# Hybrid attention and state-space trunk on one core: background sums behind products of P and V, output-projection preparation behind the last softmax, two background steps a unit

## The chip, the core and the metric

One core of a Trainium2 chip runs the whole program: TensorE (PE, with weight loads as PEld), VectorE (DVE), ScalarE (ACT), GpSimd (POOL) and SyncE (SP), which issues most DMAs. The metric is the device time of one execution in microseconds. The kernel before took 2346.74 us (median of three runs, 2342.58 to 2348.49).

## What is computed

Two layers on 1024 tokens of 1024 features, everything in float32. Layer 0 mixes tokens by latent attention, layer 1 by a state-space model; each mixer and each feed-forward network is wrapped with a modulation that depends on one vector c.

```python
cs = silu(c)
for i in range(2):
    shift, scale, gate = modulation(cs, mod_mix_w[i], mod_mix_b[i])   # cs @ W + b, W 1024 x 3072
    y = mixer_i(x * (1 + scale) + shift)
    x = layer_norm(ALPHA * x + (1 + gate) * y, ln_mix_g[i], ln_mix_b[i])
    shift, scale, gate = modulation(cs, mod_ffn_w[i], mod_ffn_b[i])
    a = relu((x * (1 + scale) + shift) @ mlp_w1[i] + mlp_b1[i])       # 1024 -> 4096
    y = (a * a) @ mlp_w2[i] + mlp_b2[i]                               # 4096 -> 1024
    x = layer_norm(ALPHA * x + (1 + gate) * y, ln_ffn_g[i], ln_ffn_b[i])
```

In the attention of layer 0, `s = q k^T` is causal, `p = softmax(s)`, `o = p v` for 8 heads, and `o @ w_o` is the output projection. The change touches only this stage and the modulation work that runs beside it.

## The kernel before

Products of float32 accuracy are made of three TensorE products: each operand is split into a high and a low part (`split`, lines 73 to 75: ACT writes the high part, DVE subtracts for the low one), and `mm3` (lines 77 to 80) adds high by high, high by low, low by high in PSUM.

**Attention.** 16 units of work are walked in order: head h (8) by half I of the queries (2), four query tiles of 128 rows each. For unit n the loop at line 800 interleaves: the projections of Q and K of unit n + 2 (`proj`), the scores of unit n + 1 (`score`), the projection of V of unit n + 1 (`vproj`), and the product of P and V of unit n (`pv`). A score tile has up to 1024 columns; its softmax is a chain over engines: DVE adds the mask (line 750) and takes the maximum (752), ACT takes the exponential (754), DVE the reciprocal of the sum (755), ACT scales the tile in place (759; for the first two tiles of a head POOL does it, line 757). `pv` transposes the scaled tile on PE (770), ACT and DVE split it (774, 775), and three products per 128 keys (782) go into PSUM tile `o`. Projections, V and the sums named next share one PSUM tile `pj` with a single buffer (line 537).

**Background.** The modulation rows of later stages are made by a generator `bg` that runs beside attention: 8 halves of 512 columns, each as 8 loads of a 128x512 block (`mb`, line 572, two raw buffers), scaled and added on POOL (574, 576, 577) into an accumulator `acc` (two buffers, so half n + 2 overwrites half n). A step of the generator is two blocks. When a half is complete, `mod_end` adds the bias (591, rows only) and sums over partitions with ones on PE: one product for a row (594) and four products of one column each (602) for columns. Halves 0, 1 give the row `grow`, 2 to 5 columns, 6 and 7 the row `gffn`. The sum of a half is written one half later than its blocks. Line 819 takes 3 steps a unit (2 in the first three units).

**Output projection.** `out_weight` (921) loads the 8 blocks of `w_o` (`wor`, 512 KB each, two buffers) and splits them into `woh`, `wol`; `o_stage` (952) splits the attention output oT into `oh` for each token tile; `o_tiles` (930) multiplies, k outermost for the first two token tiles. Block k = 7 needs the last head, so it comes after the last product of P and V.

**Order.** The instructions are written in program order, and a scheduler puts them on each engine by a simulated time line; `tc.issue_after(x)` keeps what is written under it behind instruction x. Every engine, and the SP queue with its loads, then works in that fixed order.

Of the kernel before, what the change touches and what calls it, by code (L numbers as in the profile page):

```python
# [12 lines left out]
AF = mybir.ActivationFunctionType  # L13
# [26 lines left out]
def kernel(  # L40
# [13 lines left out]
    V, S, P, PE, SY = nc.vector, nc.scalar, nc.gpsimd, nc.tensor, nc.sync  # L54
# [22 lines left out]
    def mm3(ps, lh, ll, rh, rl, start, stop):  # L77
        PE.matmul(ps, lh, rh, start=start, stop=False)  # L78
        PE.matmul(ps, lh, rl, start=False, stop=False)  # L79
        PE.matmul(ps, ll, rh, start=False, stop=stop)  # L80

    cst = pool("cst")
    ident = cst.tile([128, 128], F32, name="ident")
# [1 line left out]
    ones = cst.tile([128, 128], F32, name="ones")  # L85
# [211 lines left out]
    ps = tr4()  # L297
# [172 lines left out]
    for v, vt in ((v1, vt1), (v2, vt2)):  # L470
        ps = tr4()
# [93 lines left out]
    def mod_block(wsrc, bsrc, bcols, m, kind, dst, psp, hv, drow=None, on_pool=False):  # L565

        for h in range(2):
# [14 lines left out]
            hv.flush()  # L582
            hv.pend.append(lambda h=h, acc=acc: mod_end(bsrc, bcols, m, h, kind, dst, psp, hv, acc, drow))

    def mod_end(bsrc, bcols, m, h, kind, dst, psp, hv, acc, drow):
        c0 = m * 1024 + h * 512
        sl = slice(h * 512, h * 512 + 512)
        if kind == "row":
            r = hv.raw()
            SY.dma_start(r[0:1], bsrc[c0:c0 + 512].unsqueeze(0))  # L590
            P.tensor_tensor(acc[0:1], acc[0:1], r[0:1], ALU.add)
        ps = psp()
        if kind == "row":
            PE.matmul(ps, ones, acc, start=True, stop=True)
            if drow is None:
                V.tensor_scalar(dst[:, sl], ps, 1.0, None, ALU.add)
            else:
                V.tensor_scalar(r[0:1], ps[0:1], 1.0, None, ALU.add)
                SY.dma_start(drow[:, sl], r[0:1])
        else:  # L600
            for k in range(4):
                PE.matmul(ps[:, k:k + 1], acc[:, k * 128:(k + 1) * 128], ones[:, 0:1], start=True, stop=True)
            ks = slice(4 * h, 4 * h + 4)
            V.scalar_tensor_tensor(dst[:, ks], ps[:, 0:4], 1.0 if m == 1 else 0.0, bcols[:, ks], ALU.add, ALU.add)

# [21 lines left out]
    def step(gen, n=1, late=0):  # L627
        if late:
            with tc.high_priority(offset=-late):
                step(gen, n)  # L630
            return
        for _ in range(n):
            next(gen, None)
# [3 lines left out]
    bg = chain(mod_block(mod_mix_w[0], mod_mix_b[0], None, 2, "row", grow, pj, hv, on_pool=True),  # L637
               mod_all(0, mod_ffn_w[0], mod_ffn_b[0], 48, 0, 0, gffn, pj, hv, on_pool=True), mod_flush(hv))
# [87 lines left out]
        yield  # L726

    PT = {}
    behind_ = []

    def score(h, i):
        I = i // 4
        w = (i + 1) * 128
        ps = ps_s[i % 2].tile([128, 1024], F32, tag="s", name="s")
        qsl = slice((i % 4) * 128, (i % 4) * 128 + 128)
        qh, ql = Q[h, I]
        st = ST[h, I]
        for cc in range((w + 511) // 512):
            n = min(512, w - 512 * cc)
            if n == 128:  # L740
                n = 256
            o = ps[:, 512 * cc:512 * cc + n]
            kh, kl = K_[h, cc]
            mm3(o, qh[:, qsl], ql[:, qsl], kh[:, 0:n], kl[:, 0:n], True, False)
            ks, kx = (kE, kO) if h % 2 == 0 else (kO, kE)
            ksl = slice(512 * cc, 512 * cc + n)
            PE.matmul(o, st[:, qsl], ks[:, ksl], start=False, stop=False)
            PE.matmul(o, st[:, qsl], kx[:, ksl], start=False, stop=True)
        d = ps[:, i * 128:i * 128 + 128]
        V.tensor_tensor(d, d, cmask, ALU.add)  # L750
        mx = ap3.tile([128, 16], F32, tag="mx", name="mx", bufs=4)
        V.reduce_max(mx[:, 1:2], ps[:, 0:w], axis=AX.X, negate=True)
        p = ap3.tile([128, w], F32, tag=f"p{i}", name="p", bufs=1)
        S.activation(p, ps[:, 0:w], AF.Exp, bias=mx[:, 1:2], scale=1.0, accum_out=mx[:, 2:3])
        V.reciprocal(mx[:, 3:4], mx[:, 2:3])
        if i < 2:
            behind_.append(P.tensor_scalar(p, p, mx[:, 3:4], 0.0, ALU.mult, ALU.add).ins)
        else:
            S.activation(p, p, AF.Copy, scale=mx[:, 3:4])
        PT[h, i] = p  # L760

    def pv(h, I):
        hp, hh = divmod(h, 2)
        o = ps_o.tile([128, 512], F32, tag="o", name="o")
        nk = 4 * I + 4
        for kt in range(nk):
            j0 = max(kt - 4 * I, 0)
            tp = tr4()
            for j in range(j0, 4):
                PE.transpose(tp[:, j * 128:j * 128 + 128], PT[h, 4 * I + j][:, kt * 128:kt * 128 + 128], ident)  # L770
            ph = ap3.tile([128, 512], F32R, tag="ph", name="ph", bufs=5)
            pl_ = ap3.tile([128, 512], F32R, tag="pl", name="pl", bufs=5)
            c0 = j0 * 128
            S.activation(ph[:, c0:512], tp[:, c0:512], AF.Copy)
            V.tensor_tensor(pl_[:, c0:512], tp[:, c0:512], f32(ph[:, c0:512]), ALU.subtract)
            if j0 == 3:
                c0 = 256
                V.memset(f32(ph[:, 256:384]), 0.0)
                V.memset(f32(pl_[:, 256:384]), 0.0)
            vh, vl = VV[hp, kt // 2]  # L780
            vsl = slice((kt % 2) * 256 + hh * 128, (kt % 2) * 256 + hh * 128 + 128)
            mm3(o[:, c0:512], vh[:, vsl], vl[:, vsl], ph[:, c0:512], pl_[:, c0:512], kt == 0, kt == nk - 1)
            yield
        S.activation(oT[I][:, h].rearrange("p (s n) -> p s n", s=8), o.rearrange("p (n s) -> p s n", s=8), AF.Copy)

# [14 lines left out]
    for n, (h, I) in enumerate(units):  # L800
        pr = proj(*units[n + 2]) if n + 2 < len(units) else iter(())
        vp = vproj(*units[n + 1]) if n + 1 < len(units) else iter(())
        pvg = pv(h, I)
        for i in range(4):
            s_ = 4 * n + 4 + i
            if s_ < len(tiles):
                if s_ // 4 == n + 2:
                    step(pr, 100)
                score(*tiles[s_])
            step(pvg, 1 if I == 0 else 2)  # L810
            step(pr)
            if i > 1:
                step(vp)
        step(pvg, 100)
        step(pr, 100)
        if n + 3 < len(units) and units[n + 3][0] % 2 == 0:
            qpe(units[n + 3][0] // 2, units[n + 3][1])
        with tc.issue_after(behind_[1]):
            step(bg, 3 if n > 2 else 2)
    step(bg, 100)  # L820
    for I in range(2):
        tap(f"oT{I}", oT[I])
    for p_ in (*ps_s[::-1], ps_o, ps_j, pt_, bg_p, ap3, ap2, ap1, mk, mp):
# [97 lines left out]
    def out_weight(wp, src, gate, k, hi, lo):  # L921

        r = wp.tile([128, 1024], F32, tag="wr", name="wor")
        d = SY.dma_start(r, src[k * 128:(k + 1) * 128, :])
        if gate is not None:
            V.tensor_tensor(r, r, gate, ALU.mult)
        split(hi, lo, r)
        return d.ins

    def o_tiles(lhs, w, k_outer=False):  # L930
# [4 lines left out]
        for i, hf, k in order:  # L935
# [5 lines left out]
    wp = pool("wp", bufs=2)  # L941
    wo_p = [pool(f"wo_p{i}") for i in range(3)]
    wo_k = [wo_p[0 if k < 2 else 1 if k < 7 else 2] for k in range(8)]
    WO = [(wo_k[k].tile([128, 1024], F32R, name=f"woh{k}"), wo_k[k].tile([128, 1024], F32R, name=f"wol{k}"))
          for k in range(8)]
    for k in range(8):
        out_weight(wp, mla_w_o[0], None, k, *WO[k])
    rb = res_row(wp, ln_mix_b[0], gb2=(gffn, mlp_b2[0]))
    tok = lambda ap: ap[0].rearrange("(n t) d -> t n d", t=8)
    xr = tok(x)  # L950
# [1 line left out]
    def o_stage(t):  # L952

        if t % 2 == 0:
            hl = [wp.tile([128, 8, 128], F32R, tag=g, name="oh", bufs=1) for g in ("k4", "a4")]
        elif t in (3, 5):
            hl = [wp.tile([128, 8, 128], F32R, tag="wr", name="oh") for _ in range(2)]
        else:
            hl = [wp.tile([128, 4, 128], F32R, tag="r2", name="oh", bufs=4) for _ in range(4)]
        n = 16 // len(hl)  # L960
        parts = [(k0, k0 + n) for k0 in range(0, 8, n)]
        if t < 2:
            parts = [(a, b) for p_ in parts for a, b in ((p_[0], min(p_[1], 7)), (7, p_[1])) if a < b]
        for a, b in parts:
            i = 2 * (a // n)
            for I in range(2):
                sl = slice(64 * I, 64 * I + 64)
                ks = slice(a % n, a % n + b - a)
                split(hl[i][:, ks, sl], hl[i + 1][:, ks, sl],
                      oT[I].rearrange("p h (s n) -> p h s n", s=8)[:, a:b, t], P if t > 2 else V)  # L970
        return lambda k: (hl[2 * (k // n)][:, k % n], hl[2 * (k // n) + 1][:, k % n])
# [138 lines left out]
        mm2(js, 0)  # L1110
        mm2(js, 1)

    lhs = [o_stage(0), o_stage(1)]
    for t in range(8):
        SY.dma_start(X[t], xr[t])
    ps01 = o_tiles(lhs, WO.__getitem__, True)
# [483 lines left out]
```

## Time and profile before

| | us |
|---|---|
| median of three runs | 2346.74 |
| profiled execution | 2342.66 |
| its span | 2340.9 |
| attention units, from the first background block to the last product of P and V | about 100 to 389 |
| output projection of the first two token tiles | 359 to 395 |
| feed-forward networks, the state-space mixer and the rest | 405 to 2341 |

The profile gives busy time by engine, a chain of waits followed back from the last instruction, waits by pair of instructions, and time lines. The granted clock (PEclk) is the share of full speed at which the matrix array was clocked. Lost time of TensorE in a stretch is used below as idle time plus busy time times one minus the granted clock.

### The profile page before, as it was taken

The page shows a single profiled execution, that of the slowest core. Times are in us where ns is not written, and L with a number is a line of the kernel's source. Part 1 is how long each engine was busy: PE and PEld are TensorE (multiplying, and loading weights), DVE is VectorE, ACT ScalarE, POOL GpSimd, SP SyncE. Part 2 cuts the span into 40 slices and gives each one's busy share as a digit, 9 for nine tenths or more (in the row PEclk, how much of TensorE's full clock was granted, in tenths as well). Part 3 has the DMA queues.
Part 4 walks back from the last instruction along what each step waited for, and adds up shares of the span by engine and source line. Part 5 has one row for each costly group of instructions (what it writes and reads, how often), then busy time and mean ns, then how long its engine had stood idle before and what let it go on. Part 6 is the DMA issues. An engine that isn't in the chain of part 4 may idle for free.

```text
span 2340.9 us, 29191 instructions
## 1 busy us (share of the span) xinstructions
PE 2238.6 (96%) x11063; PEld 1881.8 (80%) x11063; DVE 1385.2 (59%) x2411; ACT 822.6 (35%) x1401; POOL 623.3 (27%) x735
## 2 busy tenths in 40 slices
PE   8899988989999999999998999999999999999996
PEld 7678866867888888888788998877788888888885
DVE  7877755466777876766443445454644444444437
ACT  3667654352222233332335233325222222322321
POOL 5467742270010144334020113534400000000005
PEclk9999998999999999999999999999999999999998
DMA  7123323114455255445413564320211111211201
GB/s 252 53 84 93 95 73 135 28 63 144 144 172 161 55 142 141 135 123 136 100 73 135 163 203 140 108 81 28 73 60 38 53 56 36 61 48 37 63 27 72
DMA packets 190444, 227.36 MB, mean 97 GB/s; under 512 B 45242, under 2 KB 136645, under 8 KB 188255
## 3 DMA queue, kind: packets, MB, share of 16 engines
q1 hardware_dynamic: 185422, 212.90, 29.6%
q0 software_dynamic: 3840, 12.59, 1.8%
q8 instruction: 87, 1.43, 0.3%
q14 instruction: 55, 0.44, 0.1%
q10 hardware_dynamic: 1040, 0.00, 0.0%
HBM read 188.80 MB, written 34.54 MB: 95 GB/s over the span
## 4 chain that ended last, share of the span: by engine, by line
PE 80%; DVE 9%; DMA 5%; ACT 2%; issue 1%; POOL 1%; SPq 1%; DVEq 0%; ACTq 0%; POOLq 0%
PE mm L78 12%; PE mm L79 12%; PE mm L80 12%; PE a L78 11%; PE a L79 11%; PE a L80 11%; PE mm L1419 1%; DMA mb<-in_mod_mix_w_dram 1%; PE tr L770 1%; DMA w2r<-in_mlp_w_dram 1%; DVE w2r L1027 1%; DVE pb L75 1%; DMA wor<-in_ssm_w_out_dram 1%; DVE macc L341 1%; PE a L1446 1%
## 5 line engine op out<-in xcount | busy, mean ns | idle before, releaser
L848 DVE TENSOR_TENSOR X<-X,mm 128x512 f32<-128x512 f32 x478 | 324.1, 684 | 287.9 <-PE mm L80 284.5
L78 PE MATMUL mm<-pb 128*128 128x512 f32 x512 | 202.2, 397 | 4.8 <-DVE X L848 4.8
L78 PE MATMUL a<-hT,pb 128*128 128x512 f32 x496 | 195.4, 394 | 6.9 <-DVE pb L1055 6.9
L79 PE MATMUL mm<-pb 128*128 128x512 f32 x512 | 200.3, 392 | 0.0
L80 PE MATMUL mm<-pb 128*128 128x512 f32 x512 | 200.1, 391 | 0.0
L79 PE MATMUL mm<-ct 128*128 128x512 f32 x512 | 199.7, 390 | 0.0
L80 PE MATMUL mm<-ct 128*128 128x512 f32 x512 | 199.6, 390 | 0.0
L78 PE MATMUL mm<-ct 128*128 128x512 f32 x512 | 198.8, 390 | 0.0
L78 PE MATMUL a<-hT,ct 128*128 128x512 f32 x496 | 194.2, 391 | 4.6 <-DVE ct L1055 4.6
L1052 ACT ACTIVATE a<-a,vt 128x512 f32<-128x512 f32 x128 | 83.4, 652 | 324.5 <-PE a L80 324.5
L79 PE MATMUL a<-hT,ct 128*128 128x512 f32 x496 | 193.7, 391 | 0.0
L80 PE MATMUL a<-hT,ct 128*128 128x512 f32 x496 | 193.5, 390 | 0.0
L80 PE MATMUL a<-hT,pb 128*128 128x512 f32 x496 | 193.4, 390 | 0.0
L79 PE MATMUL a<-hT,pb 128*128 128x512 f32 x496 | 193.3, 390 | 0.0
L904 POOL TENSOR_TENSOR X<-X,rb 128x1024 f32<-128x1024 f32 x6 | 14.7, 2473 | 638.7 <-ACT X L880 638.7
L1027 DVE TENSOR_TENSOR w2r<-w2r,gffn 128x1024 f32<-128x1024 f32 x64 | 89.3, 1397 | 130.7 <-DMA w2r<-in_mlp_w_dram 130.6
L78 PEld LDWEIGHTS mm<-pb 128*128 128x128 f32 x512 | 96.4, 188 | 27.7 <-DVE X L848 7.7
L78 PEld LDWEIGHTS a<-hT,pb 128*128 128x128 f32 x496 | 93.3, 188 | 28.2 <-DVE pb L1055 8.6
L78 PEld LDWEIGHTS a<-hT,ct 128*128 128x128 f32 x496 | 93.5, 189 | 25.2 <-DVE ct L1055 5.9
L80 PEld LDWEIGHTS mm<-ct 128*128 128x128 f32 x512 | 96.5, 189 | 20.2
L80 PEld LDWEIGHTS mm<-pb 128*128 128x128 f32 x512 | 96.4, 188 | 20.3
L78 PEld LDWEIGHTS mm<-ct 128*128 128x128 f32 x512 | 96.3, 188 | 20.3 <-ACT ct L74 0.5
(505 smaller groups left out, 5349.2 us busy)
## 6 DMA issues: line engine op xcount, KB each, us to landing
w1r<-in_mlp_w_dram SPq DMA_DIRECT2D x64, 512.0 KB, 4.1
w2r<-in_mlp_w_dram SPq DMA_DIRECT2D x64, 512.0 KB, 3.7
pt<-prm_d SPq DMA_DIRECT2D x16, 1536.0 KB, 9.1
prm_d<-cb SPq DMA_DIRECT2D x80, 128.0 KB, 2.5
wm<-in_mod_mix_w_dram SPq DMA_DIRECT2D x8, 1024.0 KB
mb<-in_mod_ffn_w_dram POOLq DMA_DIRECT2D x32, 256.0 KB, 3.1
mb<-in_mod_ffn_w_dram SPq DMA_DIRECT2D x32, 256.0 KB, 3.0
mr<-in_mod_ffn_w_dram SPq DMA_DIRECT2D x32, 256.0 KB, 3.6
```

The source lines that it names most:

```text
L75: (eng or V).tensor_tensor(lo, src, f32(hi), ALU.subtract)
L78: PE.matmul(ps, lh, rh, start=start, stop=False)
L79: PE.matmul(ps, lh, rl, start=False, stop=False)
L80: PE.matmul(ps, ll, rh, start=False, stop=stop)
L341: V.scalar_tensor_tensor(a, w[:, kc, sl], csT[:, kc:kc + 1], a, ALU.mult, ALU.add)
L770: PE.transpose(tp[:, j * 128:j * 128 + 128], PT[h, 4 * I + j][:, kt * 128:kt * 128 + 128], ident)
L848: V.tensor_tensor(xh, xh, ps[h], ALU.add)
L904: P.tensor_tensor(X[t], X[t], ra, ALU.mult)
L1027: V.tensor_tensor(r, r, gate, ALU.mult)
L1052: S.activation(ps, ps, AF.Relu, bias=vt2[:, l * 32 + j:l * 32 + j + 1])
L1419: PE.matmul(pvv[i][:, g * 128:g * 128 + 128], pt[:, i, g], ug[:, g], start=True, stop=True)
L1446: PE.matmul(o, zc[:, g], pt[:, 2, g], start=False, stop=True)
```

## The change

`mm3` returns its last instruction; `pv` keeps it in a list; `mod_end` writes its sums on PE under `issue_after` of the latest entry; the last reciprocal and the last scaling of a tile are kept, and the eight `out_weight` calls and `o_stage(0)`, `o_stage(1)` are written under `issue_after` of both; the background takes 2 steps in every unit. The lines behind the first edit move by up to 15 in the new file (594 becomes 590, 602 becomes 593, 759 becomes 771, 924 becomes 937).

```diff
@@ mm3
-        PE.matmul(ps, ll, rh, start=False, stop=stop)
+        return PE.matmul(ps, ll, rh, start=False, stop=stop).ins
@@ background
+    pe_last = []
+
+    def mod_sum(ps, acc, kind):
+        if kind == "row":
+            PE.matmul(ps, ones, acc, start=True, stop=True)
+        else:
+            for k in range(4):
+                PE.matmul(ps[:, k:k + 1], acc[:, k * 128:(k + 1) * 128], ones[:, 0:1], start=True, stop=True)
...
         ps = psp()
+        if pe_last:
+            with tc.issue_after(pe_last[-1]):
+                mod_sum(ps, acc, kind)
+        else:
+            mod_sum(ps, acc, kind)
         if kind == "row":
-            PE.matmul(ps, ones, acc, start=True, stop=True)
...
         else:
-            for k in range(4):
-                PE.matmul(ps[:, k:k + 1], acc[:, k * 128:(k + 1) * 128], ones[:, 0:1], start=True, stop=True)
@@ score
-        V.reciprocal(mx[:, 3:4], mx[:, 2:3])
+        r_ = V.reciprocal(mx[:, 3:4], mx[:, 2:3])
...
-            S.activation(p, p, AF.Copy, scale=mx[:, 3:4])
+            sm_last[:] = r_.ins, S.activation(p, p, AF.Copy, scale=mx[:, 3:4]).ins
@@ pv
-            mm3(o[:, c0:512], vh[:, vsl], vl[:, vsl], ph[:, c0:512], pl_[:, c0:512], kt == 0, kt == nk - 1)
+            pe_last.append(mm3(o[:, c0:512], vh[:, vsl], vl[:, vsl], ph[:, c0:512], pl_[:, c0:512], kt == 0, kt == nk - 1))
@@ unit loop
         with tc.issue_after(behind_[1]):
-            step(bg, 3 if n > 2 else 2)
+            step(bg, 2)
     step(bg, 100)
+    pe_last.clear()
@@ output projection
-    for k in range(8):
-        out_weight(wp, mla_w_o[0], None, k, *WO[k])
+    with tc.issue_after(sm_last[0]), tc.issue_after(sm_last[1]):
+        for k in range(8):
+            out_weight(wp, mla_w_o[0], None, k, *WO[k])
...
-    lhs = [o_stage(0), o_stage(1)]
+    with tc.issue_after(sm_last[0]), tc.issue_after(sm_last[1]):
+        lhs = [o_stage(0), o_stage(1)]
```

The scheduler decides where the rows go. On PE, in the second half of head 6, the sum of half 6 stood between products of P and V (`o`), ahead of the projection of Q for the last head (`pj<-cqh,wqh`). Before:

```order
L770 MATMUL tr_3810<-ident,p 128x128 x4
L79 MATMUL o<-pl,vh 128x512
L80 MATMUL o<-ph,vl 128x512
L770 MATMUL tr_3822<-ident,p 128x128 x4
L594 MATMUL pj<-mb_1008,ones 128x512
L78 MATMUL o<-ph,vh 128x512
```

Now both row sums of `gffn` stand behind the very last product of P and V, ahead of block 7 of the output projection:

```order
L78 MATMUL o<-ph,vh 128x256
L79 MATMUL o<-pl,vh 128x256
L80 MATMUL o<-ph,vl 128x256
L590 MATMUL pj<-mb_1008,ones 128x512 x2
L78 MATMUL mm<-woh_4185,oh 128x512 x4
L79 MATMUL mm<-wol_4186,oh 128x512 x4
```

The sums no longer stand ahead of the projection; the sum of half 5 moved behind the product of P and V of unit 14, just ahead of the last transposes.

On ACT, at the end of the last softmax (the tile with 1024 columns), the splits of attention output (`oh`) and of weight block 0 (`woh_4171`) stood ahead of the exponential and of the scaling. Before:

```order
L754 ACTIVATE p,mx<-s,mx 128x896
L74 ACTIVATE oh<-oT 128x7x64 x2
L74 ACTIVATE oh<-oT 128x64
L74 ACTIVATE oh<-oT 128x4x64 x2
L754 ACTIVATE p,mx<-s,mx 128x1024
L759 ACTIVATE p<-p,mx 128x896
L74 ACTIVATE oh<-oT 128x3x64 x2
L74 ACTIVATE oh<-oT 128x64
L74 ACTIVATE woh_4171<-wor 128x1024
L759 ACTIVATE p<-p,mx 128x1024
```

Now they stand behind it:

```order
L766 ACTIVATE p,mx<-s,mx 128x896
L771 ACTIVATE p<-p,mx 128x896
L786 ACTIVATE ph<-tr_3977 128x128
L766 ACTIVATE p,mx<-s,mx 128x1024
L796 ACTIVATE oT<-o 128x512
L771 ACTIVATE p<-p,mx 128x1024
L74 ACTIVATE woh_4171<-wor 128x1024
L74 ACTIVATE oh<-oT 128x7x64 x2
L74 ACTIVATE oh<-oT 128x4x64 x2
```

Nothing of the output projection stands between the last exponential and its scaling any more; the store of unit 14's output (`oT`) does.

On SP, the loads of the output weights (`wor`) stood behind all background loads (`mb`). Before:

```order
L572 DMA mb_1009<-in_mod_ffn_w_dram 128x512 x12
L590 DMA mb_1009<-in_mod_ffn_b_dram 1x512 x2
L924 DMA wor<-in_mla_w_o_dram 128x1024 x2
L910 DMA rb<-in_ln_mix_b_dram 128x1024
L924 DMA wor<-in_mla_w_o_dram 128x1024 x6
```

Now the two kinds alternate, with six blocks of half 7 among the weights:

```order
L572 DMA mb_1009<-in_mod_ffn_w_dram 128x512 x10
L937 DMA wor<-in_mla_w_o_dram 128x1024 x2
L923 DMA rb<-in_ln_mix_b_dram 128x1024
L572 DMA mb_1009<-in_mod_ffn_w_dram 128x512 x2
L937 DMA wor<-in_mla_w_o_dram 128x1024
L572 DMA mb_1009<-in_mod_ffn_w_dram 128x512
L937 DMA wor<-in_mla_w_o_dram 128x1024
```

Each weight load moved behind a background load, which in turn waits for POOL to free a raw buffer.

More of the change, by code (lines that the diff above doesn't have):

```diff
@@ L728 @@
     PT = {}
-    behind_ = []
+    behind_, sm_last = [], [None, None]
     def score(h, i):
```

## The prediction, made before the changed kernel ran

> **What bounds the kernel now.** I read the page's busy times first, then a table of stretches around the change, then the time lines of single places.
>
> ```profile
> PE 2238.6 (96%) x11063; PEld 1881.8 (80%) x11063; DVE 1385.2 (59%) x2411; ACT 822.6 (35%) x1401; POOL 623.3 (27%) x735
> ```
>
> PE is busy for 96% of the span. The change neither adds nor removes a product (eight sums stay eight sums), so a gain can only come from PE idling less, or from fewer products at a reduced clock. The order of work differs between the kernels from the second unit or so, near 170 us, up to the output projection. The view by stretches shows what can be lost there. Its columns are the stretch, its length, busy time of PE, weight loads, DVE, ACT and POOL, granted clock, DMA share and GB/s.
>
> ```profile
> 100.00:170.00 70.00, 63.39 (x339) 52.69 (x338) 56.17 (x113) 49.04 (x100) 46.03 (x55) 0.98 0.30 85
> 170.00:310.00 140.00, 132.74 (x764) 113.13 (x762) 108.39 (x232) 97.48 (x198) 103.20 (x119) 1.00 0.32 93
> 310.00:353.60 43.60, 36.19 (x184) 28.43 (x183) 22.06 (x53) 21.62 (x44) 13.64 (x15) 0.96 0.17 56
> 353.60:365.00 11.40, 6.83 (x23) 4.97 (x22) 7.92 (x17) 9.69 (x19) 0.00 (x0) 0.70 0.25 74
> 365.00:389.00 24.00, 23.65 (x113) 18.91 (x111) 9.37 (x13) 7.88 (x14) 6.95 (x4) 1.00 0.35 118
> 389.00:405.00 16.00, 10.67 (x26) 8.07 (x27) 10.79 (x25) 4.11 (x9) 5.37 (x9) 0.68 0.69 264
> ```
>
> Lost time (idle plus busy times one minus the clock) is 7.9 us in the first row, 7.3 in the second, 7.41 + 1.45 = 8.9 in the third, 4.57 + 2.05 = 6.6 in the fourth, 0.35 in the fifth. So the change has some 15 us within reach between 310 and 365, and 7 us that it may lose or gain in the middle.
>
> **(a) The sums, 310 to 353.6.** Of the eight sums only that of half 6 held PE:
>
> ```profile
> 322.24 1.31 PE L594 MATMUL pj<-mb,ones 128*128 128x512 f32 x2 [3.05 <-POOL mb L591]
> ...
> 323.77 0.63 PE L79 MATMUL o<-pl,vh 128*128 128x512 f32 x1
> 324.19 0.63 PE L80 MATMUL o<-ph,vl 128*128 128x512 f32 x1
> ```
>
> PE waited 3.05 us for POOL's addition of the bias. Behind it products start 0.42 us apart, and the clock is the next cost. For comparison, a shorter wait later:
>
> ```profile
> 348.88 0.50 PE L78 MATMUL s<-kh,qh 128*128 128x512 f32 x1 [1.46 <-ACT p L754]
> 349.22 0.40 PE L79 MATMUL s<-kl,qh 128*128 128x512 f32 x1
> 349.45 0.39 PE L80 MATMUL s<-kh,ql 128*128 128x512 f32 x1
> ```
>
> Here the distance is 0.23 us, so 0.42 is about half speed. In the order of the change this sum stands behind the last product of P and V, and the projection of Q for the last head no longer queues behind it for `pj`; what is late next in this stretch is the softmax. If the stretch then runs like 170 to 310, with 7.3/140 = 5.2% lost, 2.3 us remain: **+6.6** (gains count positive). If only the wait goes, +3; if all goes, +8.9. I take +6.6, since the second row is the same kind of units with sums that never wait.
>
> **(b) The preparation behind the last softmax, 353.6 to 365.** PE's last score, transposes, and first product of the output projection:
>
> ```profile
> 353.12 0.40 PE L748 MATMUL s<-kE,stO 128*128 128x512 f32 x1
> 353.36 0.60 PE L770 MATMUL tr<-ident,p 128*128 128x128 f32 x4
> 357.61 0.69 PE L770 MATMUL tr<-ident,p 128*128 128x128 f32 x2 [3.66 <-ACT p L759]
> 359.21 1.22 PE L78 MATMUL mm<-woh,oh 128*128 128x512 f32 x2 [0.91 <-ACT woh L74]
> ```
>
> It idles 3.66 us, then 0.91. What it waits for, on ACT and DVE:
>
> ```profile
> 353.75 1.79 ACT L74 ACTIVATE oh<-oT 128x448 fp32r<-128x448 f32 x5
> 355.44 1.10 ACT L754 ACTIVATE p<-s,mx 128x1024 f32<-128x1024 f32 x1
> ...
> 356.53 1.03 ACT L759 ACTIVATE p<-p,mx 128x896 f32<-128x896 f32 x1
> 357.46 0.75 ACT L74 ACTIVATE oh<-oT 128x192 fp32r<-128x192 f32 x3
> 358.11 1.05 ACT L74 ACTIVATE woh<-wor 128x1024 fp32r<-128x1024 f32 x1
> 359.06 1.15 ACT L759 ACTIVATE p<-p,mx 128x1024 f32<-128x1024 f32 x1
> ```
>
> ```profile
> 353.55 0.30 DVE L750 TENSOR_TENSOR s<-s,cmask 128x128 f32<-128x128 f32 x1 [0.90 <-PE s L748]
> 353.89 1.23 DVE L752 TENSOR_REDUCE mx<-s 128x1 f32<-128x1024 f32 x1
> ```
>
> The maximum is done at 355.1, but the scaled tile only at 360.2: 1.79, 1.03, 0.75 and 1.05 us of ACT stand in its way, of which 4.6 lie outside the chain and all but the scaling of the earlier tile belong to the output projection. Behind the change ACT's chain from the last score (353.5) is 0.30 + 1.23 + 1.10, a store of unit 14's output that now stands between (512 columns, 0.6 as an estimate from half of the 1024-column row), and 1.15: 4.4 us, with handoffs about 4.8. Ahead of the last transposes the new order leaves PE some 3.5 us of products of unit 14, transposes and sums of columns, so it idles 1.3. Then the output projection must start: `woh` 1.05 and two `oh` of about 0.56 (from 448 columns), 2.2 us, behind which the transposes give only 0.2 of cover: 2.0 idle. Nothing hides these splits any more; they are the price of the new place. Half speed afterwards may cost 2.4 us (the stretch's 2.05 is its like); at even odds 1.2. Lost 4.5 instead of 6.6: **+2.1**. Bounds: 0 (the idle time only moves behind the softmax) to +3.3 (full clock).
>
> The clock between these gaps has a row on either side: 1.46 us of idle left it full, 3.05 did not, and this one is between as well:
>
> ```profile
> 390.73 1.58 PE L78 MATMUL mm<-woh,oh 128*128 128x512 f32 x4 [1.77 <-ACT oh L74]
> 392.11 1.91 PE L79 MATMUL mm<-wol,oh 128*128 128x512 f32 x4
> ```
>
> Four products here take 1.38 to 1.70 us to the next row, against 0.92 at 0.23 each: reduced after 1.77 us. The Trainium skill ("TensorE: Matmul & The Clock Gate", Part 1, The HAM clock gate) says that the array falls to half clock after at least one idle window of about 3.4 us and is released after about 3.4 us of sustained work. By that rule neither gap of (b) would reduce it, and the sum would be 1.2 us better. The row at 390.73 speaks against it, since half speed followed a shorter gap; I keep even odds.
>
> **(c) The first weights behind POOL.** The SP queue now issues the first two `wor` behind ten loads of `mb`, which wait until POOL frees a raw buffer; half 6 starts on POOL only when the sum of half 4 has freed the accumulator.
>
> ```profile
> 301.23 0.70 POOL L574 TENSOR_SCALAR mb<-mb,csT 128x512 f32<-128x512 f32 x1 [0.80 <-PE pj L80]
> ...
> 319.71 1.26 POOL L577 TENSOR_TENSOR mb<-mb,mb 128x512 f32<-128x512 f32 x1
> ```
>
> ```profile
> 104.35 1.21 POOL L574 TENSOR_SCALAR mb<-mb,csT 128x512 f32<-128x512 f32 x1 [2.40 <-DMA mb<-in_mod_mix_w_dram]
> ...
> 126.43 1.30 POOL L577 TENSOR_TENSOR mb<-mb,mb 128x512 f32<-128x512 f32 x1
> ```
>
> ```profile
> wor<-in_mla_w_o_dram SPq DMA_DIRECT2D x8, 512.0 KB, 3.6
> ```
>
> A half took 19.7 us (301.23 to 320.97), at worst 23.4 (104.35 to 127.73), and a weight lands 3.6 after its issue. From the sum of half 4 that is about 1 + 19.7 + 0.4 + 3.6 = 24.7 us. From the same sum the order gives PE 78 products (18 us) and 27 transposes, about 20 us to the last score, and (b) 4.8 more: 24.8. Just in time; with the slow half the weights are 3.7 late and the clock drops, a dozen products at 0.2 more, 2.5. I take **-1.0**; bounds 0 and -6.2. The six loads behind them alternate with `mb` loads, see the last rival.
>
> **(d) Row sums in the gap before block 7.** Ahead of 390.73 PE sat idle 1.77 us. Both row sums move there. One costs about 0.85 us of PE at full clock:
>
> ```profile
> 336.57 1.02 PE L594 MATMUL pj<-mb,ones 128*128 128x512 f32 x2
> 337.03 0.68 PE L80 MATMUL o<-ph,vl 128*128 128x256 f32 x1
> 337.55 0.28 PE L78 MATMUL o<-ph,vh 128*128 128x256 f32 x1
> ```
>
> (0.98 from the first to the third row, less some 0.13 for the product between.) So 1.7 us leave the stretches above; the two with a read of the single `pj` between need about 2.4, 0.6 more than the gap: +1.1. The clock may stay up behind them for block 7, whose twelve products lose about 1.8 now: a third of that. **+1.6**, bounds -0.6 and +2.9.
>
> **(e) The middle, 170 to 310.** Two steps a unit instead of three spread POOL's work, which is far from late there by the same 19.7 us a half. But products of P and V now stand closer behind their splits, and the tile of 1024 columns has 5.3 to 6.6 us of PE work (rows counted at 0.23 each) to hide its chain of 4.4 and the split, where it had 6.1 to 11.4. The kernel before already waits there:
>
> ```profile
> L79 PE MATMUL o<-pl,vh 128*128 128x512 f32 (+2 forms) x53 | 19.4, 365 | 4.1 <-DVE pl L775 4.0
> ```
>
> Four waits of 1 us; I add 0.4 at four places: **-1.5**. Bounds: the 11.3% of the first stretch would be -8.5, no loss at all +7.3.
>
> **Sum.** 6.6 + 2.1 - 1.0 + 1.6 - 1.5 = 7.8. The profiled execution took 2342.66 (span 2340.9 and 1.8 around it) and would take 2334.9. It lies 4 us below the median of the runs, so against the median I forecast 2346.7 - 7.8 = **2339**.
>
> **Rivals.** *Nothing net (0.27).* Only one sum in eight ever held PE, and the wait it caused may reappear at the softmax, as 348.88 shows already. Then (a) is +3, (b) +1, (c) -1, (d) +1, (e) -2.5: 1.5 gained, 2345. Against it: the whole stretch from 310 lost four times as much a microsecond as the middle.
> *A larger gain (0.16).* The clock stays up through the tail and no wait follows the sum: 8.9 + 3.3 + 0 + 2.9 + 3 in the middle (less than half of its 7.3) = 18, so 2329. For it: the fifth stretch, where PE lost 0.35 in 24 us. Against it: the end of the softmax keeps its chain of 4.4.
> *Slower, weights at POOL's pace (0.16).* Before, six weight loads issued in a row:
>
> ```profile
> 360.44 16.18 SPq L924 DMA_DIRECT2D wor<-in_mla_w_o_dram  x6
> ```
>
> ```profile
> mb<-in_mod_ffn_w_dram SPq DMA_DIRECT2D x13, 256.0 KB, 3.1
> ```
>
> five steps of 3.17 us. Now each stands behind an `mb` load, which waits for POOL. If these go singly, a landing of 3.1 and POOL's 2.0 (0.70 + 1.26) make 5.1 a step, 9.7 later over five; products of the last unit cover about half: 4.8. With the first pair 3.7 late and 2.5 of reduced clock this is 11.0 lost, of which (a), (b), (d) and (e) at the values of the second case give 2.5 to 8.8 back: at their low end, 8.5 slower, 2355; at the high end, 2 slower, 2349. I write 2350. It decides when a half takes POOL more than about 20 us from the sum of half 4. Against it: two raw buffers let loads run ahead, and then a step is a half's 19.7/8 = 2.5, less than 3.17.
>
> **How the numbers follow.** My forecast has 0.41, with 2331 to 2345 as its own range. A measurement of this kernel tells a change from none at about 0.3%, 7 us: faster is below 2339.7, slower above 2353.8. The forecast stands just below the first bound, so 0.25 of its 0.41 goes to faster and 0.16 to the same; the larger gain gives 0.16 to faster; nothing net gives 0.05 and 0.22; the last gives 0.09 to the same and 0.07 to slower; the loss bound of (e) reaches slower too, 0.05 from the same. Faster 0.46, same 0.42, slower 0.12. The range 2327 to 2351 holds the three likelier cases and half of the last.
>
> **What would show each step.** (a) No wait of PE for POOL at the sum, full-speed starts around it, and a loss of about 2 us in the 43 before the last score. (b) Two gaps, at the last transposes and before the first `woh` product, of 1 to 2 us each instead of 3.66 and 0.91, with the clock of the next products telling the even odds. (c) The first `wor` issue at or before the last score; if the first output product waits for a DMA, this term is wrong. (d) Two sums behind the last product of P and V, and a wait before block 7 of under 1 us. (e) 170 to 310 within 2 us of its length; waits at `pl` at 5 to 6 us. The whole is wrong if the softmax turns out to take up all that the sum gave, or if products of the output projection wait for `wor` in the 24 us after their start.

## The result

| | us |
|---|---|
| before, median of 16 runs (2340.13 to 2360.30) | 2345.35 |
| changed, median of 16 runs (2325.14 to 2345.52) | 2331.51 |
| ratio, with 95% interval | 0.9937 (0.9920 to 0.9954) |
| span of the profiled execution, before and changed | 2340.9 and 2323.4 |

The change makes the kernel faster by 0.6%, 14 to 15 us, where 7.8 us were forecast. The time of 2331.5 lies in the forecast's own range of 2331 to 2345, but only 0.5 us inside its lower end.

**The profile after.** Stretches of the changed kernel, with the columns of the table before (PE, weight loads, DVE, ACT, POOL busy, clock, DMA share, GB/s):

```profile
170.00:280.00 110.00, 104.17 (x587) 87.81 (x586) 83.08 (x175) 75.74 (x153) 63.82 (x76) 1.00 0.25 71
280.00:290.00 10.00, 9.71 (x40) 9.01 (x41) 6.07 (x19) 5.28 (x11) 3.40 (x5) 0.51 0.21 52
290.00:310.00 20.00, 20.00 (x116) 17.34 (x115) 15.99 (x33) 15.39 (x34) 15.26 (x17) 1.00 0.28 86
310.00:342.00 32.00, 31.46 (x190) 27.41 (x188) 21.68 (x53) 22.43 (x47) 16.03 (x18) 1.00 0.32 99
342.00:353.00 11.00, 8.95 (x33) 6.92 (x33) 10.31 (x15) 7.94 (x17) 9.82 (x7) 0.69 0.56 181
353.00:375.00 22.00, 21.63 (x107) 17.58 (x106) 11.15 (x17) 7.25 (x12) 15.79 (x13) 1.00 0.56 180
```

Up to the last softmax (310 to 342) PE now idles 0.54 us at full clock, where the kernel before lost 8.9 us in 310 to 353.6. One new loss stands in the middle: from 280 to 290 the clock was 0.51, which is 4.8 us.

The last softmax and the start of the output projection, on PE:

```profile
338.94 0.39 PE L760 MATMUL s<-kE,stO 128*128 128x512 f32 x1
...
341.79 0.95 PE L593 MATMUL pj<-ones,mb 128*128 128x1 f32 x8
342.61 0.53 PE L782 MATMUL tr<-ident,p 128*128 128x128 f32 x3
343.75 0.44 PE L782 MATMUL tr<-ident,p 128*128 128x128 f32 x2 [0.61 <-ACT p L771]
345.62 1.22 PE L78 MATMUL mm<-woh,oh 128*128 128x512 f32 x2 [1.44 <-ACT oh L74]
346.64 1.05 PE L79 MATMUL mm<-wol,oh 128*128 128x512 f32 x2
347.49 0.63 PE L78 MATMUL mm<-woh,oh 128*128 128x512 f32 x1
347.92 0.63 PE L79 MATMUL mm<-wol,oh 128*128 128x512 f32 x1
```

The gaps are 0.61 and 1.44 us (3.66 and 0.91 before). Behind them products start 0.43 apart, half speed, up to about 351.3. The end of attention:

```profile
374.89 0.28 PE L80 MATMUL o<-ph,vl 128*128 128x256 f32 x1
375.01 1.02 PE L590 MATMUL pj<-mb,ones 128*128 128x512 f32 x2
376.90 1.10 PE L590 MATMUL pj<-mb,ones 128*128 128x512 f32 x2 [0.87 <-DVE gffn L610]
377.43 1.49 PE L78 MATMUL mm<-woh,oh 128*128 128x512 f32 x4
378.76 1.08 PE L79 MATMUL mm<-wol,oh 128*128 128x512 f32 x4
379.68 1.07 PE L80 MATMUL mm<-woh,oh 128*128 128x512 f32 x4
385.06 0.47 PE L78 MATMUL mm<-woh,oh 128*128 128x512 f32 x1 [4.31 <-DVE X L993]
```

The last product of P and V starts at 374.89, before at 388.68: 13.8 us earlier. The first product behind the wait for `X` starts at 385.06, before at 398.94: 13.9 us. So the gain is made ahead of the last product. The remaining 3.6 us between the two spans lie behind 385. The profiled execution of the changed kernel was the fastest of its 16 (2325.14), and its second profile took 2.4 us longer behind the same product (1940.8 against 1938.3 us; 1942.0 before). So two executions of one kernel differ there by 2.4 of the 3.6 us.

**Where on the way.** Since the order on PE differs, I marked times by work done: products of the PE time line from 90 us on, counted at 0.2275 us per 512 columns and 0.075 per transpose, sums left out. The table gives the time between marks of 100, 180, 205 and 230 us of work (about 211, 308, 347 and 382 us in the kernel before) and then to the product behind the wait for `X` (398.94). Some records are missing and marks fall inside groups of rows, so a single cell is good to about 1.5 us, in the first column to about 4.

| | 100 to 180 | 180 to 205 | 205 to 230 | 230 to X | X reached at |
|---|---|---|---|---|---|
| before | 96.8 | 38.8 | 34.8 | 16.9 | 398.94 |
| changed | 99.6 | 28.6 | 32.8 | 14.6 | 385.06 |
| changed, second profile | 98.7 | 28.7 | 33.9 | 15.7 | 386.13 |

The gain sits in one place, the 25 us of work around the old sum of half 6: 10.2 us. Twelve experiments ask which part of the change made it.

### The profile page after: what moved, and what is told of

It is laid out like the page before. It is cut to its first block, busy times and chain, and to the rows that moved or that the text cites. A ratio compares the mean times of both kernels' runs of the same rounds, so it can differ in the third digit from the quotient of the medians.

```text
span 2323.4 us, 29176 instructions
## 1 busy us (share of the span) xinstructions
PE 2233.1 (96%) x11063; PEld 1879.7 (81%) x11063; DVE 1383.2 (60%) x2411; ACT 821.8 (35%) x1401; POOL 630.2 (27%) x735
## 4 chain that ended last, share of the span: by engine, by line
PE 81%; DVE 9%; DMA 4%; ACT 2%; issue 2%; SPq 1%; POOL 0%; DVEq 0%; ACTq 0%; POOLq 0%
PE mm L78 12%; PE mm L79 12%; PE mm L80 12%; PE a L78 11%; PE a L80 11%; PE a L79 11%; PE mm L1434 1%; PE tr L782 1%; DMA mb<-in_mod_mix_w_dram 1%; DMA w2r<-in_mlp_w_dram 1%; DVE pb L75 1%; DVE w2r L1041 1%; DMA qs<-qr 1%; PE o L79 1%; PE s L78 1%
## 5 line engine op out<-in xcount | busy, mean ns | idle before, releaser
L78 PEld LDWEIGHTS mm<-pb 128*128 128x128 f32 x512 | 96.3, 188 | 28.1 <-DVE X L861 7.3
L78 PEld LDWEIGHTS a<-hT,pb 128*128 128x128 f32 x496 | 94.0, 190 | 28.1 <-DVE pb L1069 8.2
L80 PEld LDWEIGHTS mm<-pb 128*128 128x128 f32 x512 | 96.4, 188 | 20.4
L79 PEld LDWEIGHTS mm<-pb 128*128 128x128 f32 x512 | 96.5, 189 | 19.5 <-issue 0.5
```

The costliest lines, as they stand in the source:

```text
L80: return PE.matmul(ps, ll, rh, start=False, stop=stop).ins
```

## The experiments

Every part alone and in combination is tried first, then the lateness of the background by itself. In the texts on record, theory A says that half 6 came too early for POOL and that its late sum is the loss; B that the order of the sums matters; C that the preparation does; P and N that the preparation costs something, or nothing.

**1. Two steps a unit alone.** The kernel before, with one line changed:

```diff
-            step(bg, 3 if n > 2 else 2)
+            step(bg, 2)
```

> Two background steps a unit alone; sums on PE unordered, preparation of the output projection not tied to the softmax. Theory A (the stretch from 308 us was lost because the background came to half 6 too early for POOL: its sum stood among the products of unit 13 and held PE 3.05 us, then starved the softmax of unit 15): the later half alone moves that sum far behind, so most of the gain of 14.8 us appears: ratio 0.995 to 0.997, no wait of PE for POOL at the sum. Theory B (ordering the sums behind products is what matters, the number of steps only spreads POOL): ratio 0.999 to 1.001.

Measured: 2336.11 us, ratio 0.9970 (0.9950 to 0.9990). The ratio is at the slow end of what theory A expected, and the gain of 8 us is half of the whole, not most of it. The stretch of work from 180 to 205 shrinks to 28.9 us and no sum waits for POOL. But the part behind it is longer than before (36.8 us from 205 to 230). Its waits of PE, in the view by pairs from 165 to 400:

```profile
PE s L78 <- ACT p L766: 3.7, 3, 2.0
PE o L79 <- DVE pl L787: 3.6, 2, 1.9
...
PE o L78 <- ACT oT L796: 3.1, 4, 1.6
PE mm L78 <- ACT oh L74: 2.1, 2, 1.8
```

Columns are the pair, the total, the number and the longest. The three waits of the first line lie ahead of 290 us. In the tail stand 1.63 us for the store of `oT` (at 344.66), 1.92 for `pl` (at 347.07) and 1.38 for `woh` (at 360.10), with half speed from 345.84 to 352.66. So the tail has new waits that take some of the gain back.

**2. The order of the sums alone.** Three steps as before, `issue_after` in `mod_end` kept.

> Sums on PE ordered behind products of P and V, alone; three steps a unit and the preparation as before. Theory A: the sum of half 6 moves only a few products further back, behind those of its own unit, and is still in front of the projection of Q of the last unit; PE still waits for POOL there, 1 to 3 us, and the ratio is 0.998 to 1.000. Theory B: the wait is gone and the ratio is 0.996 or lower.

Measured: 2346.58 us, ratio 1.0003 (0.9987 to 1.0019). Theory B falls. PE's waits from 310 to 353.6 and the place:

```profile
PE pj L590 <- POOL mb L601: 5.3, 1, 5.3
PE tr L782 <- ACT p L771: 1.7, 1, 1.7
```

```profile
329.34 2.04 PE L590 MATMUL pj<-mb,ones 128*128 128x512 f32 x2 [5.27 <-POOL mb L601]
```

The sum moved a few rows and still waited, longer (5.27 us for 3.05): the tie is to the latest product written so far, and half 6 is written while POOL still has to make it. The expectation of 1 to 3 us for this wait was too small.

**3. The preparation alone.**

> Preparation of the output projection behind the last softmax, alone. Both theories: the gap ahead of the last transposes falls from 3.66 us to about 1, that ahead of the first output product grows from 0.91 to 1.5 to 2.5; the ratio is 0.999 (2 us), 0.998 to 1.001. Theory C (the tail is where the gain comes from): 0.996 or lower.

Measured: 2344.33 us, ratio 0.9995 (0.9979 to 1.0012). Theory C falls. The first expectation was wrong too: the gap ahead of the last transposes did not go.

```profile
363.12 0.47 PE L782 MATMUL tr<-ident,p 128*128 128x128 f32 x2 [3.44 <-ACT p L771]
364.16 0.69 PE L782 MATMUL tr<-ident,p 128*128 128x128 f32 x2 [0.56 <-ACT p L771]
366.04 1.22 PE L78 MATMUL mm<-woh,oh 128*128 128x512 f32 x2 [1.19 <-ACT oh L74]
```

PE idles 3.44, 0.56 and 1.19 us, against 3.66 and 0.91 with the splits in front. From the end of the last score to the scaled tile ACT and DVE now take 4.9 us instead of 6.7, and PE has only four transposes to fill them: with nothing to do for PE, the softmax itself is as long as the gap.

**4. Sums and steps, preparation as before.** The changed kernel without its `issue_after` around `out_weight` and `o_stage`.

> The change without its middle part: sums ordered and two steps, preparation as before. Theory A and B: the ratio of the whole change, 0.9937, plus what the preparation is worth, about 0.001: 0.994 to 0.996. Theory C: 0.998 or more, since the preparation is what gains.

Measured: 2324.66 us (5 runs), ratio 0.9910 (0.9887 to 0.9933): not slower than the whole change, as I had expected, but if anything faster. So it was run again beside the changed kernel.

**5 and 6. The changed kernel and number 4 on one chip.**

> The changed kernel beside the change without its preparation part, on one chip. Theory P (the preparation behind the softmax costs time once the sums and steps have made cover for the softmax): this one is 2 to 5 us slower than the other, at 0.993 to 0.995 of the kernel before. Theory N (it is worth nothing either way, the earlier difference is noise): both within 1.5 us.

> The change without its preparation part again. Theory P: 0.990 to 0.992, no PE wait over 1 us between the last score and the last product of P and V, and full clock there. Theory N: 0.993 to 0.995, the same as the changed kernel beside it.

Measured: the changed kernel 2332.26 us, ratio 0.9945 (0.9925 to 0.9966); without the preparation 2328.99 us, ratio 0.9933 (0.9909 to 0.9957). The difference, 3.3 us, is theory P's, but the intervals overlap, and 0.9933 by itself lies in the range that was written for theory N (0.993 to 0.995) and not in P's (0.990 to 0.992). Of the 54 pairs of one run of each, the kernel without the tie was faster in 46. The trace of number 6 tells more. Around its last transposes:

```profile
341.36 0.39 PE L79 MATMUL o<-pl,vh 128*128 128x256 f32 x1 [0.91 <-DVE pl L787]
342.52 0.57 PE L782 MATMUL tr<-ident,p 128*128 128x128 f32 x3
342.80 2.00 PE L78 MATMUL mm<-woh,oh 128*128 128x512 f32 x4
344.72 0.80 PE L79 MATMUL mm<-wol,oh 128*128 128x512 f32 x1
...
348.29 0.38 PE L782 MATMUL tr<-ident,p 128*128 128x128 f32 x2
```

The products of the output projection themselves fill the wait of the softmax: the last transposes (348.29) come after sixteen of them and wait for nothing. This is what the preparation ahead of the softmax is good for once the tail is in step. The full clock that I expected was not there at first (half speed from 342.87 to 346.28); in number 4 it was.

**7. Halves 6 and 7 late, sums ordered, no tie of the preparation.** Three steps a unit as before until half 5 is done, none for three units, then two:

```diff
-            step(bg, 2)
+            step(bg, 2 if n < 3 else 3 if n < 9 else 0 if n < 12 else 2)
```

> Sums ordered, preparation as before, and steps as before (three) up to half 5, none for three units, then two: only halves 6 and 7 come later, POOL and PE up to unit 9 as with three steps. Theory A (lateness of half 6 and its sum among the products of units 13 and 14 is the whole loss): the gain of the version with two steps everywhere, 0.990 to 0.993. Theory M (two steps gain by the calmer middle too): 0.994 to 0.997, with the middle as long as before.

Measured: 2326.30 us, ratio 0.9925 (0.9899 to 0.9951), in theory A's range.

**8. The same without the order of the sums.** Neither of the other two parts of the change is in it: the sums are not ordered and the preparation is not tied.

> As the last, without the order of the sums; the order on PE is that of the kernel before up to unit 9. The sums of halves 6 and 7 fall among the products of the output projection. Theory A: no wait of PE for POOL at the sums, last score some 10 us earlier than before; ratio 0.995 to 0.997 like two steps alone, since the tail's softmax still lacks cover. Theory M: 0.998 to 1.000.

Measured: 2327.07 us, ratio 0.9927 (0.9905 to 0.9949). This is the clean test of theory A, and it came out faster than theory A had said. Delaying the writing of two halves, and nothing else, gives the whole gain in time. (POOL's work and the loads of these halves move with their sums; no run moves a sum alone.) No sum waits for POOL, and the last score starts at 335.78, 17.3 us earlier than before, where some 10 were expected; two waits behind it, 2.84 us for `pl` and 3.12 for `woh`, give part of that back. Theory M, by which the calmer middle has a share, falls. The ratio is also better than that of two steps alone (0.9970, 0.9950 to 0.9990), though half 6 is late in both: what two steps in every unit cost beside the delay, no run isolates.

**9. More steps instead of fewer.**

> The kernel before with four background steps a unit instead of three (from unit 3 on). Theory A (a background written faster than POOL's 19.7 us a half lets sums on PE arrive ahead of their data): the sums stand still earlier on PE and wait longer for POOL, at least 6 us over several sums; ratio 1.002 to 1.010. Theory D (only the position of half 6 beside the last units hurts, since products before it have cover): the sums wait little and the tail is free of background; ratio 0.993 to 0.997.

Measured: 2360.99 us, ratio 1.0070 (1.0055 to 1.0086). Waits of PE from 240 to 345:

```profile
PE tr L782 <- ACT p L771: 10.4, 3, 6.3
PE pj L593 <- POOL mb L577: 2.8, 1, 2.8
PE pj L590 <- POOL mb L601: 2.1, 1, 2.1
```

The direction and the ratio are theory A's, though the waits at sums are 4.9 us and not 6. The larger bill comes at the softmax: 10.4 us in three waits, the longest 6.34. The first 80 us of work from mark 100 took 131.0 us. A sum that holds the single `pj` holds the projections queued for it, and the scores and softmax that need these come without products around them; that link between the rows is my reading, since no run took the two apart.

**10. Two steps and the preparation, sums unordered.**

> The change without the order of the sums: two steps and the preparation behind the softmax. Theory P (preparation behind the softmax is worth nothing or costs): 0.996 to 0.998, like two steps alone (0.997). Theory Q (it is needed where no sums fill the end of the softmax): 0.993 to 0.995, without the waits of 1.6 to 2.0 us on ACT that two steps alone had at the store of unit 14 and the splits.

Measured: 2336.52 us, ratio 0.9963 (0.9948 to 0.9977), like two steps alone. Theory Q falls: the waits at the store of unit 14 shrank, but those at `oh` grew.

**11 and 12. Number 7 with the preparation tied to the softmax, and number 7 again, on one chip.**

> Halves 6 and 7 late, sums ordered, and the preparation behind the softmax. Beside the next kernel it shows what the preparation is worth. Theory P: 2 to 5 us slower than the next, with gaps of about 0.6 us at the last transposes and 1.4 ahead of the first output product and half clock behind them. Theory N: within 1.5 us.

> Halves 6 and 7 late and sums ordered, preparation as before, again: 0.990 to 0.994 by theory A, faster than the changed kernel's 0.994 in the same place as last time.

Measured: 2326.75 us, ratio 0.9933 (0.9909 to 0.9958), against 2323.08 us, ratio 0.9909 (0.9895 to 0.9924). The difference of 3.7 us is theory P's again, and the trace of number 11 has the gaps that it named, 0.62 and 1.44 us with half speed behind them. By the intervals alone it is still not settled; of the 36 pairs of runs the kernel without the tie was faster in 31.

**All of it by work done** (marks as above):

| | 100 to 180 | 180 to 205 | 205 to 230 | 230 to X | X reached at |
|---|---|---|---|---|---|
| sums alone | 97.6 | 44.7 | 35.1 | 18.3 | 404.89 |
| preparation alone | 101.7 | 39.0 | 35.7 | 19.7 | 406.08 |
| steps alone | 101.9 | 28.9 | 36.8 | 16.5 | 392.66 |
| steps, preparation | 100.5 | 29.0 | 35.3 | 17.5 | 392.63 |
| sums, steps | 100.9 | 28.1 | 29.8 | 15.7 | 386.78 |
| sums, steps, again | 99.0 | 28.4 | 30.6 | 15.7 | 381.58 |
| halves 6 and 7 late | 95.3 | 29.0 | 38.1 | 16.1 | 387.91 |
| the same, sums | 94.7 | 28.9 | 31.1 | 16.3 | 379.53 |
| the same, sums, again | 96.1 | 28.9 | 30.4 | 16.2 | 384.43 |
| the same, sums, preparation | 95.3 | 29.0 | 32.7 | 17.1 | 385.26 |

Three readings. From 180 to 205 there are two groups, 38.8 to 44.7 us where half 6 comes early and 28.1 to 29.0 where it comes late, whatever else is changed. From 205 to 230 there are three: 34.8 to 38.1 without ordered sums behind a late half, 32.7 to 33.9 with ordered sums and the preparation behind the softmax, 29.8 to 31.1 with ordered sums and the preparation left free. So in that stretch, one profile for each kernel, the order of the sums is worth 5 to 7 us where the preparation is left free, and the tie of the preparation costs 2 to 4. In total time the order shows with two steps a unit (2336.11 against 2324.66 us, experiments 1 and 4) and not with delayed halves (2327.07 against 2326.30, experiments 8 and 7). From 100 to 180, two steps a unit took 98.7 to 101.9 us and the delayed halves 94.7 to 96.1; but the preparation alone, with the same order on PE as before up to that point, took 101.7 against 96.8, and the same products stood 1.3 us behind the kernel before at 206 us and 4.6 behind it at 306. So a single execution moves by over 3 us there and no more is claimed.

One thing stays open. The three kernels with late halves and unordered sums were late at X (387.91 to 392.66) and yet their spans (2324.2 to 2329.2) are near those of the others: they took 1935.9 to 1936.5 us behind X, the ten others 1938.3 to 1943.1. The order of the engines differs behind X too, and no run separates this.

**The version to take** is number 7: two runs of it gave 2326.30 and 2323.08 us, ratios 0.9925 (0.9899 to 0.9951) and 0.9909 (0.9895 to 0.9924), faster than the kernel before, and below the changed kernel's 2331.51 and 2332.26 (0.9937 and 0.9945), with intervals that overlap or come within 0.0001 of it. Numbers 4, 6 and 8 (2324.66, 2328.99 and 2327.07) cannot be told from it.

## Why the prediction was right, and where it was not

The direction, the place and the range held. The size was 14 to 15 us for 7.8.

**(a) The sums, +6.6.** Right about the place and the wait, and mis-sized. Experiment 8 shows that the loss there came from writing half 6 too early. In the kernel before, 3.05 us of it are the wait at the sum and 1.7 the half speed behind it (323.05 to 326.46; the 1.45 of the prediction rests on a rounded clock); that the rest are waits which follow from these is argued and not taken apart by a run. The step of the prediction that failed is "If the stretch then runs like 170 to 310, with 7.3/140 = 5.2% lost, 2.3 us remain". The stretch kept 0.54 us, not 2.3, so that its loss of 8.9 nearly all went: +8.4, close to the "if all goes" bound. Counted by work done the stretch gained 10.2, of which 1.7 are the two sums that moved out (booked under (d)): 8.5. The prediction gave the credit to the wrong part, the order by which "this sum stands behind the last product of P and V": that order alone does not move the sum out of the way (experiment 2), the later writing does. With two steps a unit the later writing alone was worth half the gain (experiment 1) and the order the rest (experiment 4); with delayed halves the writing was worth all of it (experiment 8).

**(b) The preparation, +2.1.** The numbers came out, the reason only in part. Predicted gaps of 1.3 and 2.0 us, measured 0.61 and 1.44, and the two terms of the first gap held: the chain from the last score to the scaled tile took 4.4 us (4.4 to 4.8 forecast) and PE had 3.8 us of other work under it (3.5 forecast); the loss of the stretch fell from 6.6 to 2.05 + 2.77 = 4.8 us (342 to 353), where 4.5 had been forecast. But "1.79, 1.03, 0.75 and 1.05 us of ACT stand in its way" names the wrong thing as what has to go. With those splits moved alone the gap stayed (3.44, experiment 3); with them left in place, under ordered late sums, it vanished (experiments 4 and 6), since PE then has products of the output projection to run while the softmax ends. So it was the cover on PE that decided, which came with the order and lateness of the sums and not with the preparation. "Nothing hides these splits any more; they are the price of the new place" was right, and by both comparisons on one chip the price is larger than what the place brings. The even odds on the clock fell to half speed, in both profiles of the changed kernel.

**(c) First weights, -1.0.** The time held, the cost did not come.

```profile
337.80 0.86 SPq L937 DMA_DIRECT2D wor<-in_mla_w_o_dram  x2
```

The first `wor` was issued 1.1 us before the last score, as the sum had it, and ACT began its split at 343.58 behind the softmax and not behind a transfer. From 353 to 375 PE idled 0.37 us: no weight held it. The slower rival, weights at POOL's pace, fell in time but not in mechanism: the last six weight loads were issued between 346.08 and 364.71, steps of 3.7 us instead of 3.17 (5.1 by the rival, 2.5 by its counter-argument), and ACT sat idle 11.7 us for five of them. PE had products of the last unit to run meanwhile.

**(d) Row sums in the gap, +1.6.** Right: net of the sums 0.1 us was gained from the last product to X, where -0.1 had been forecast. PE reached block 7 2.26 us behind the end of the last product instead of 1.77, 0.5 later where 0.6 was forecast, with 0.87 us of it for DVE's read of the single `pj`. The clock stayed up: block 7's twelve products took 3.3 us instead of 4.6. But the next wait grew from 3.61 to 4.31 us, since it is for `X` on DVE: half of that clock gain went there.

**(e) The middle, -1.5.** Not settled. The two profiles lost 2 to 3 us by work done, no more than the cells of the first column are good for, and the preparation alone moved 3.4 us there, product by product, with the same order on PE. The clock took 4.8 us between 280 and 290, which the sum had no term for. Waits at `pl` did not grow to 5 to 6 us; they are 3.1 and 2.6.

**The sum.** By work done: +2.1 ahead of mark 100 and -2.8 to mark 180 for the -1.5 of (e); +10.2 for the 6.6 of (a) and the 1.7 of moved sums; +2.0 for the 1.1 of (b) and (c); +2.3 behind mark 230. Of this only 0.1 is (d), for -0.1 forecast, since the last product came 13.8 us earlier and X 13.9; the other 2.2 have no term in the sum and are hardly more than the cells are good for. That is 13.8 measured for 7.8, the shift of X in one profile of each kernel. The differences all point the same way and add up to 6.0 us, so that the time stayed in the range by 0.5 us was luck. The rival "nothing net" fell with experiment 8. The "larger gain" of 18 us rested on full clock through the tail and on a gain in the middle, and neither came.

## What to carry to other kernels

Where background work feeds a sum on the bounding engine, it should not be written faster than the engine that prepares it can follow: around one sum of 0.85 us that came too early some 8 us were lost here. That most of this is what queues behind the sum and loses its cover for the softmax is my reading of the rows. An order tie (`issue_after`) moves a consumer only behind what has been written already, so it does not mend a producer that is written too early. And before moving preparation out of the way of a softmax, look at what PE can run meanwhile: here the moved preparation was itself the source of that cover, and in both comparisons on one chip the kernel with it left alone was the faster, by 3.3 and 3.7 us, each with overlapping intervals.

## What the runs showed of the clock

The granted clock fell to half after shorter gaps than the 3.05 us at the old sum. Ahead of the slow stretch from 280 to 290:

```profile
277.81 0.45 PE L79 MATMUL o<-pl,vh 128*128 128x384 f32 x1 [1.32 <-DVE pl L787]
278.10 0.34 PE L80 MATMUL o<-ph,vl 128*128 128x384 f32 x1
278.27 0.38 PE L782 MATMUL tr<-ident,p 128*128 128x128 f32 x2
279.41 0.43 PE L78 MATMUL s<-kh,qh 128*128 128x256 f32 x1 [0.76 <-ACT p L766]
```

Two gaps of 1.32 and 0.76 us with a few products between brought half speed for about 10 us. In the kernel before, two longer gaps left it full:

```profile
291.70 0.50 PE L79 MATMUL o<-pl,vh 128*128 128x512 f32 x1 [1.19 <-DVE pl L775]
...
295.45 0.50 PE L79 MATMUL o<-pl,vh 128*128 128x512 f32 x1 [1.64 <-DVE pl L775]
295.78 0.39 PE L80 MATMUL o<-ph,vl 128*128 128x512 f32 x1
296.01 0.60 PE L770 MATMUL tr<-ident,p 128*128 128x128 f32 x4
```

So it is not the longest gap that decides. In all fourteen profiles the granted clock changes only at instants that lie a whole number of steps of 3.41 us apart (in the kernel before at 323.05, 326.46, 357.18 and 364.01: 1, 9 and 2 steps). Between such instants, in the view by stretches, first the kernel before, then the changed one:

```profile
288.92:292.33 3.41, 2.22 (x13) 1.58 (x12) 3.41 (x5) 0.60 (x1) 3.33 (x3) 1.00 0.22 55
292.33:295.74 3.41, 1.77 (x10) 1.25 (x9) 3.38 (x7) 2.13 (x5) 2.80 (x3) 1.00 0.34 99
295.74:299.16 3.42, 3.42 (x19) 2.83 (x19) 3.36 (x7) 3.09 (x7) 3.15 (x4) 1.00 0.25 77
```

```profile
276.20:279.61 3.41, 1.33 (x7) 0.76 (x5) 3.31 (x6) 3.21 (x6) 0.94 (x2) 1.00 0.28 84
279.61:283.02 3.41, 2.99 (x11) 2.30 (x11) 3.22 (x11) 3.06 (x7) 0.15 (x1) 0.50 0.27 62
```

The longer pair of gaps fell into two steps, with 1.19 and 1.64 us idle, and the clock stayed full; the shorter pair fell into one, with 2.08, and it dropped. From 100 us on the fourteen profiles hold 139 such drops from full clock: 124 behind a step with at least 1.7 us idle, half of it. Only 16 steps at full clock with that much idle were not followed by a drop, none of them with 1.95 or more. The drop behind the last softmax (344.46) is one of the exceptions: its step had 0.90 us idle, and much of its busy time was transposes and products of one column. The Trainium skill ("TensorE: Matmul & The Clock Gate", Part 1, The HAM clock gate) gives at least one idle window of about 3.4 us; the traces here show the drop when such a step was idle for about half of its length.
